# Where a two-layer encoder kernel issues its adding DMAs, builds its operand differences, and computes its last gates

## The chip, the cores and the metric

One core of a Trainium2 chip runs the whole kernel in one launch. The metric is device time in microseconds (us) of that launch. Engines are named as in the profile: PE is TensorE (matrix multiply), DVE is VectorE, ACT is ScalarE, POOL is GpSimd, SP is SyncE, which here only issues DMAs. Each engine works through its own instructions strictly in order; semaphores tie the engines together.

## The reference

The input x is 512 tokens by 1024, in float32. Layer 0 is a pooling mixer of inner width 2048 in 4 groups of 512:

```
hn = rms_norm(x)
v, gate = split(hn @ w_in)                       # 1024 -> 2 x 2048
p[g] = mean of v[g] over the last 2, 4, 8, 16 tokens - v[g]
x = x + ((p[g] @ w_grp[g]) * scale * silu(gate)) @ w_out
```

Layer 1 is a gated linear recurrence (HGRN2) of 16 heads of 128, followed by a final norm:

```
q, f, i, gate = split(rms_norm(x) @ w_in)        # 1024 -> 4 x 2048
o = recurrence over tokens, decay from f, key from f, value i, query q
x = x + (rms_norm(o, per head) * silu(gate)) @ w_out
out = rms_norm(x)
```

## The kernel before, in words

**Products.** Every product keeps nearly full float32 precision: each operand is split into a rounded high part (ACT copies it, line 98) and a low remainder (DVE subtracts, line 99), and `mm3` (lines 130 to 132) issues three matmuls per step of the contraction. Weights arrive in pieces of 512 KB: SP loads `wraw` (three buffers), ACT makes `whi`, DVE makes `wlo` (six buffers each). Results gather in four PSUM banks named `mm` and four named `a`.

**Layer 0** runs over four groups g of 512 channels. `values(g)` projects and DVE scales into `v`; `pool(g)` forms the window sums by doubling, one DVE add per doubling (line 305), into a tile `win` with two buffers, of which POOL must first clear the 16 columns ahead of the tokens (line 304); the next add reads those columns. `project_out` adds the group before into the residual h. `gates0(g)` projects the gate; its last step `gs` is a POOL multiplication (line 323). `mixed(g)` multiplies by `w_grp`. The row norm is not applied to the operand but afterwards: its factor `rn_l` (line 278, POOL) is spread over a tile by eight small matmuls (line 198) in the midst of the first gate product, and every layer 0 result waits for it.

**Layer 1** runs over four groups of four heads: `inputs(g)` forms the values, `heads` the weights within blocks and the states, `attend` the outputs, `gates1` the gates, `gated` their product, `prepare(g + 1)` decay, key and query of the next group, `add_out` the output product of the group before.

**A seven-product scheme.** The values of groups 2 and 3 are computed together by `inputs2`, which treats tokens, contraction and channels in halves and uses seven products of halves in place of eight. Three of these need sums of weight quarters; `weight_sums` builds four such sums (`wsum`, w4 to w7) in HBM with DMAs issued by POOL, 512 KB each, part of which add into their destination (`accum_op=ALU.add`). Four need differences of the activations; `differences` computes d and e (128 x 512 each, for j = 0 to 3), splits them, and stores all halves in HBM (`sums_d`); `again(i)` loads the one wanted into the buffers of the residual h, which is dead by then.

**What sets the order.** A planner orders the instructions of each engine before the program runs. It simulates the engines and at each moment issues, of what it holds to be ready, the instruction that was written earliest. Weight loads and splits are given a head start. An instruction without inputs to wait for can so stand far ahead of its place in the text. `weight_sums` is such a case: written inside layer 0, its 16 DMAs need nothing but each other.

Of the kernel before, what the change touches and what calls it, by code (L numbers as in the profile page):

```python
# [32 lines left out]
F32 = mybir.dt.float32  # L33
F32R = mybir.dt.float32r
# [3 lines left out]
ALU = mybir.AluOpType  # L38
PSUM = bass.MemoryType.PSUM

P = 128
D = 1024
T = 512
# [24 lines left out]
def trunk(ctx: ExitStack, tc: tile.TileContext, xT, x_d, par, ident_d, causal_d, mask_d, fg_d, w0_in, w0_grp, w0_out, w1_in, w1_out, out):  # L68
# [164 lines left out]
    def weight_sums(step):  # L233

        for g in PAIRS:
            w5, w6, w7, w4 = (wsum[g][i] for i in range(4))
            todo = (((w5, quarter(g, 0, 0), False), (w7, quarter(g, 0, 1), False)),
                    ((w5, quarter(g, 0, 1), True), (w7, quarter(g, 1, 1), True)),
                    ((w6, w5, False),), ((w6, quarter(g, 1, 1), True),),
                    ((w4, w6, False),), ((w4, quarter(g, 1, 0), True),))[step]  # L240
            for out_, in_, adding in todo:
                for r in range(0, 4 * P, 2 * P):
                    if adding:
                        nc.gpsimd.dma_start(out=out_[r:r + 2 * P], in_=in_[r:r + 2 * P], accum_op=ALU.add)
                    else:
                        nc.gpsimd.dma_start(out=out_[r:r + 2 * P], in_=in_[r:r + 2 * P])


    with tc.tile_pool(name="l0", bufs=1) as l0:
# [88 lines left out]
        zprev = None  # L338
        for g in range(NG):
            vs = values(g)  # L340
            if g:
                weight_sums(2 * g - 2)
            px = pool(g, vs)
            if zprev is not None and g < NG - 1:
                project_out(load_out(w0_out, g - 1), zprev)
            gts = gates0(g)
            if g:
                weight_sums(2 * g - 1)
            z = mixed(g, px, gts)
            if g == NG - 1:  # L350
                project_out(load_out(w0_out, g - 1), zprev)
            zprev = z
# [24 lines left out]
    def hgrn(ctx, general, h):  # L377
# [73 lines left out]


        own = [[(hi[:, t:t + 256], lo[:, t:t + 256]) for hi, lo in xs[k:k + 4]] for t in (0, 256) for k in (0, 4)]
        sums_d = dram.tile([2, 4, P, 2, T], F32, name=f"sums_{name}")
        v_d = dram.tile([TB, P, GC], F32, name=f"v_{name}")
        nrn = l1.tile([P, TB], F32, name="nrn")
        nc.gpsimd.tensor_scalar(out=nrn, in0=rn, scalar1=-1.0, scalar2=None, op0=ALU.mult)
        def differences():
            for j in range(4):
                t0, t4 = (small.tile([P, T], F32, name="t", tag="hg", bufs=2) for _ in range(2))  # L460
                for t, k in ((t0, j), (t4, 4 + j)):
                    nc.scalar.activation(out=t, in_=h[k], func=AF.Copy, scale=pp[:, C_NG1 + k:C_NG1 + k + 1])
                d, e = (small.tile([P, T], F32, name="d", tag="sq", bufs=2) for _ in range(2))
                u, w = slice(0, 256), slice(256, 512)
                nc.vector.tensor_tensor(out=d[:, u], in0=t4[:, w], in1=t0[:, w], op=ALU.subtract)
                nc.vector.scalar_tensor_tensor(out=d[:, w], in0=d[:, u], scalar=-1.0, in1=t0[:, u], op0=ALU.mult, op1=ALU.subtract)
                nc.vector.tensor_tensor(out=e[:, u], in0=t0[:, u], in1=t0[:, w], op=ALU.subtract)
                nc.vector.scalar_tensor_tensor(out=e[:, w], in0=t4[:, u], scalar=-1.0, in1=d[:, w], op0=ALU.mult, op1=ALU.subtract)
                first = halves(d, "z1", 4, l1)
                second = [const.tile([P, T], F32R, name="s", tag=f"h{k}", bufs=1) for k in (j, 4 + j)]  # L470
                split(e, *second)
                for i, pair in enumerate((first, second)):
                    for c, x in enumerate(pair):
                        nc.scalar.dma_start(out=sums_d[i, j, :, c], in_=x.bitcast(F32))

        def again(i):

            out = []
            for j in range(4):
                x = const.tile([P, 2, 256], F32R, name="s", tag=f"h{4 * (i % 2) + j}", bufs=1)  # L480
                nc.sync.dma_start(out=x.bitcast(F32), in_=sums_d[i // 2, j, :, :, (i % 2) * 256:(i % 2) * 256 + 256])
                out.append((x[:, 0], x[:, 1]))
            return out

        def inputs2(g):

            def pieces(src):
                v = src.rearrange("(k p) n -> p k n", p=P)
                out = []
                for i in range(0, 4, 2):
                    hi, lo = piece(v[:, i:i + 2])
                    out += [(hi[:, 0], lo[:, 0]), (hi[:, 1], lo[:, 1])]
                return out
            def product(accs, x, w):
                for b, acc in enumerate(accs):  # L500
                    t = slice(b * P, (b + 1) * P)
                    for k, ((xh, xl), (wh, wl)) in enumerate(zip(x, w)):
                        mm3(acc, xh[:, t], xl[:, t], wh, wl, k == 0, k == 3)

            two = lambda: [ps.tile([P, T], F32, name="mm", tag="mm", bufs=4) for _ in range(2)]
            v = l1.tile([P, TB, GC], F32, name="vn", tag="vn", bufs=1)
            v1 = [l1.tile([P, GC], F32, name="v1", tag="gs", bufs=4) for _ in range(TB)]
            s = again

            def plus(out, acc, x):  # L510
                nc.vector.tensor_tensor(out=out, in0=acc, in1=x, op=ALU.add)

            def times(x, by, t):
                nc.scalar.activation(out=x, in_=x, func=AF.Copy, scale=by[:, t:t + 1])

            a = two()
            product(a, own[0], pieces(quarter(g, 0, 0)))
            for b in range(2):
                nc.scalar.copy(out=v[:, 2 + b], in_=a[b])
            a = two()  # L520
            product(a, own[1], pieces(quarter(g, 1, 0)))
            for b in range(2):
                plus(v[:, b], a[b], v[:, 2 + b])
                times(v[:, b], rn, b)
            c = two()
            product(c, s(0), pieces(wsum[g][0]))
            s2 = s(1)
            a = two()
            product(a, s2, pieces(wsum[g][1]))
            s3 = s(2)  # L530
            for b in range(2):
                plus(v1[b], a[b], v[:, 2 + b])
            a = two()
            product(a, s3, pieces(wsum[g][2]))
            s4 = s(3)
            for b in range(2):
                plus(v[:, 2 + b], a[b], v1[b])
                plus(v1[2 + b], c[b], v[:, 2 + b])
                plus(v1[b], c[b], v1[b])
                times(v1[2 + b], nrn, 2 + b)  # L540
                nc.scalar.dma_start(out=v_d[2 + b], in_=v1[2 + b])
            a = two()
            product(a, own[3], pieces(wsum[g][3]))
            for b in range(2):
                plus(v[:, 2 + b], a[b], v[:, 2 + b])
                times(v[:, 2 + b], rn, 2 + b)
            a = two()
            product(a, s4, pieces(quarter(g, 1, 1)))
            for b in range(2):
                plus(v1[b], a[b], v1[b])  # L550
                times(v1[b], nrn, b)
                nc.scalar.dma_start(out=v_d[b], in_=v1[b])
            return v
# [61 lines left out]
        def group(g, prepare, heads, zs):  # L615
# [2 lines left out]
            first, last = g == 0, g == NG - 1  # L618
            v = inputs(g)
            if last:  # L620
                wg = load_in(w1_in, 3 * DI + g * GC)
                gts = gates1(wg, (0, 1))
                attend = heads(g, v, lambda: gts.extend(gates1(wg, (2, 3))))
                wo = load_out(w1_out, g - 1)
                add_out(wo, zs, (0,))
                ons = [attend(n) for n in range(GT)]
                add_out(wo, zs, (1,))
            elif first:
                attend = heads(g, v)
                turn()  # L630
                differences()
                wg = load_in(w1_in, 3 * DI + g * GC)
                gts = gates1(wg, (0, 1))
                ons = [attend(n) for n in range(GT)]
                gts += gates1(wg, (2, 3))
            else:
                attend = heads(g, v)
                add_out(load_out(w1_out, g - 1), zs)
                ons = [attend(n) for n in range(GT)]
                gts = gates1(load_in(w1_in, 3 * DI + g * GC), range(GT))  # L640
            now = [gated(g, n, ons[n], gts[n], last) for n in range(2)]
            if not last:
                prepare(g + 1)
            now += [gated(g, n, ons[n], gts[n], last) for n in range(2, GT)]
            if last:
                add_out(wo, zs, (2, 3))
            return now

        def finish(zs):
# [315 lines left out]
```

## Time and profile before

| | |
|---|---|
| time, median of 3 runs | 879.32 us (877.96 to 882.0) |
| profiled execution: its own time, its span | 877.26 us, 875.3 us |
| PE busy | 820.3 us (94%) |
| DVE, ACT, POOL busy | 574.3 us (66%), 294.4 us (34%), 163.5 us (19%) |
| DMA moved | 103.18 MB, mean 118 GB/s |
| chain that ended last | PE 74%, DVE 11%, issue 7%, DMA 4% |

Busy is the share of the span in which the engine executes. The chain that ended last is followed back from the last instruction, step by step, to whatever released it. "issue" is time in which an engine waited for nothing that the profile shows.

### The profile page before, as it was taken

The page shows a single profiled execution, that of the slowest core. Times are in us where ns is not written, and L with a number is a line of the kernel's source. Part 1 is how long each engine was busy: PE and PEld are TensorE (multiplying, and loading weights), DVE is VectorE, ACT ScalarE, POOL GpSimd, SP SyncE. Part 2 cuts the span into 40 slices and gives each one's busy share as a digit, 9 for nine tenths or more (in the row PEclk, how much of TensorE's full clock was granted, in tenths as well). Part 3 has the DMA queues.
Part 4 walks back from the last instruction along what each step waited for, and adds up shares of the span by engine and source line. Part 5 has one row for each costly group of instructions (what it writes and reads, how often), then busy time and mean ns, then how long its engine had stood idle before and what let it go on. Part 6 is the DMA issues. An engine that isn't in the chain of part 4 may idle for free.

```text
span 875.3 us, 10353 instructions
## 1 busy us (share of the span) xinstructions
PE 820.3 (94%) x3878; PEld 683.9 (78%) x3878; DVE 574.3 (66%) x881; ACT 294.4 (34%) x500; POOL 163.5 (19%) x214
## 2 busy tenths in 40 slices
PE   8707999999999999999999999999998999998995
PEld 6506888888888888888788878888876888887884
DVE  3405784467368656579847996437997654896764
ACT  4502422322242324442545223324244243313321
POOL 1112100200110202226013430032410012242300
PEclk9957999999999999999999999999999999999999
DMA  9982422322242314513373333212358342212202
GB/s 319 308 213 54 130 91 92 103 69 97 97 144 78 108 59 160 177 49 97 121 258 103 96 97 97 73 33 89 97 181 273 123 145 77 89 56 80 85 1 100
DMA packets 50091, 103.18 MB, mean 118 GB/s; under 512 B 3888, under 2 KB 8240, under 8 KB 49968
## 3 DMA queue, kind: packets, MB, share of 16 engines
q1 hardware_dynamic: 41248, 83.90, 29.0%
q0 software_dynamic: 2880, 8.39, 4.1%
q10 hardware_dynamic: 5904, 10.15, 3.2%
q8 instruction: 32, 0.52, 0.2%
q14 instruction: 27, 0.22, 0.1%
HBM read 92.99 MB, written 17.83 MB: 127 GB/s over the span
## 4 chain that ended last, share of the span: by engine, by line
PE 74%; DVE 11%; issue 7%; DMA 4%; POOL 1%; ACT 1%; POOLq 0%; DVEq 0%; SPq 0%; ACTq 0%
PE mm L131 22%; PE mm L130 22%; PE mm L132 22%; DVE r L718 3%; DVE wlo L99 3%; PE a L773 2%; DMA wsum<-wsum 1%; PE a L751 1%; PE a L775 1%; DMA wraw<-wsum 1%; DMA wraw<-in_w1i 1%; PE a L734 1%; ACT whi L98 1%; DMA s<-sums_fac 1%; DVE q L722 1%
## 5 line engine op out<-in xcount | busy, mean ns | idle before, releaser
L130 PE MATMUL mm<-xh,whi 128*128 128x512 f32 x624 | 245.0, 393 | 1.9 <-ACT whi L98 1.9
L131 PE MATMUL mm<-xl,whi 128*128 128x512 f32 x624 | 243.8, 391 | 0.0
L132 PE MATMUL mm<-xh,wlo 128*128 128x512 f32 x624 | 243.7, 391 | 0.0
L98 ACT CAST whi<-wraw 128x1024 fp32r<-128x1024 f32 (+1 forms) x146 | 147.7, 1025 | 239.6 <-PE mm L131 111.8
L99 DVE TENSOR_TENSOR wlo<-wraw,whi 128x1024 fp32r<-128x1024 f32 (+1 forms) x146 | 180.2, 1258 | 52.9 <-ACT whi L98 51.0
L130 PEld LDWEIGHTS mm<-xh,whi 128*128 128x128 f32 x624 | 117.5, 188 | 26.7 <-ACT whi L98 2.6
L132 PEld LDWEIGHTS mm<-xh,wlo 128*128 128x128 f32 x624 | 117.6, 188 | 25.4 <-DVE wlo L99 0.7
L131 PEld LDWEIGHTS mm<-xl,whi 128*128 128x128 f32 x624 | 117.6, 188 | 24.0
L718 DVE RECIPROCAL r<-r 128x512 f32<-128x512 f32 x16 | 53.4, 3338 | 0.0
L130 PE MATMUL mm<-zh,whi 128*128 128x512 f32 x128 | 49.8, 389 | 0.0
L131 PE MATMUL mm<-zl,whi 128*128 128x512 f32 x128 | 49.8, 389 | 0.0
L132 PE MATMUL mm<-zh,wlo 128*128 128x512 f32 x128 | 49.8, 389 | 0.0
L407 DVE TENSOR_TENSOR ht<-mm,ht 128x512 f32<-128x512 f32 x32 | 22.0, 688 | 30.1 <-PE mm L132 30.0
L592 POOL TENSOR_TENSOR ro<-mo,mhalf 128x4 f32<-128x4 f32 x16 | 16.2, 1014 | 134.5 <-DVE mo L590 134.5
L224 DVE TENSOR_TENSOR h<-mm,h 128x512 f32<-128x512 f32 x32 | 21.9, 688 | 28.3 <-PE mm L132 28.0
L323 POOL TENSOR_TENSOR gs<-gt,sg 128x512 f32<-128x512 f32 x16 | 21.9, 1373 | 87.6 <-ACT sg L321 87.6
L130 PE MATMUL mm<-whi,z1h 128*128 128x512 f32 x96 | 37.9, 395 | 0.0
L580 POOL TENSOR_TENSOR gs<-fz,s 128x512 f32<-128x512 f32 x16 | 22.4, 1403 | 81.5 <-ACT s L578 81.3
L131 PE MATMUL mm<-wlo,z1h 128*128 128x512 f32 x96 | 37.5, 390 | 0.0
L132 PE MATMUL mm<-whi,z1l 128*128 128x512 f32 x96 | 37.5, 390 | 0.0
L293 DVE TENSOR_TENSOR v<-mm,rb 128x512 f32<-128x512 f32 x16 | 10.8, 687 | 38.5 <-ACT rb L204 30.8
L131 PE MATMUL mm<-wlo,xh 128*128 128x512 f32 x88 | 34.5, 392 | 0.8 <-DVE wlo L99 0.8
(177 smaller groups left out, 1287.2 us busy)
## 6 DMA issues: line engine op xcount, KB each, us to landing
wraw<-in_w1i SPq DMA_DIRECT2D x62, 512.0 KB, 4.1
wraw<-in_w0i SPq DMA_DIRECT2D x28, 512.0 KB, 4.6
wraw<-in_w0o SPq DMA_DIRECT2D x16, 512.0 KB, 3.9
wraw<-in_w1o SPq DMA_DIRECT2D x16, 512.0 KB, 4.5
wsum<-in_w1i POOLq DMA_DIRECT2D x12, 512.0 KB, 7.0
wraw<-in_w0g SPq DMA_DIRECT2D x8, 512.0 KB, 4.0
s<-sums_fac SPq DMA_DIRECT2D x16, 256.0 KB, 4.3
wraw<-wsum SPq DMA_DIRECT2D x8, 512.0 KB, 4.1
```

Source lines behind the costliest of these rows:

```text
L98: nc.scalar.copy(out=hi, in_=src)
L99: nc.vector.tensor_tensor(out=lo, in0=src, in1=hi, op=ALU.subtract)
L130: nc.tensor.matmul(out, lh, rh, start=start, stop=False)
L131: nc.tensor.matmul(out, lh, rl, start=False, stop=False)
L132: nc.tensor.matmul(out, ll, rh, start=False, stop=stop)
L224: nc.vector.tensor_tensor(out=h[n], in0=acc, in1=h[n], op=ALU.add)
L323: nc.gpsimd.tensor_tensor(out=gs, in0=gt, in1=sg, op=ALU.mult)
L407: nc.vector.tensor_tensor(out=ht[b][:, c], in0=acc, in1=ht[b][:, c], op=ALU.add)
L580: nc.gpsimd.tensor_tensor(out=gs, in0=gt, in1=sg, op=ALU.mult)
L592: nc.gpsimd.tensor_tensor(out=ro[:, :, 0], in0=mo, in1=mhalf[:, :TB], op=ALU.pow)
L718: nc.vector.reciprocal(out=r, in_=r)
L773: nc.tensor.matmul(o[:, b], Ads[pr][:, j, t], v[:, b, n * P:(n + 1) * P], start=True, stop=b == 0)
```

## The change

1. `weight_sums` has four steps in place of six and is called once in each group of layer 0, after `gates0(g)`. Step 0 copies (8 DMAs of 512 KB), steps 1, 2 and 3 only add (8, 4 and 2 DMAs): 22 DMAs in place of 16, and 14 of them add in place of 8. No DMA reads `wsum` as a source any more. Each is passed to `tc.keep_in_program_order`, which makes the planner place it behind the POOL instruction written just ahead of it.
2. `differences` moves from group 0 of layer 1 (behind `turn`) to group 1 (behind `attend`, ahead of the gates). The two halves of e are split and stored; the two halves of d are split into the same buffers afterwards and stay on chip in `diff`. `inputs2` uses `diff` for its first two difference products and loads only the last two (8 loads in place of 16, 8 stores in place of 16, 256 KB each, now in one contiguous 2 KB run per partition).
3. In the last group all four gates come ahead of `heads`; `add_out` of the group before, four blocks of tokens, fills the places between: block 0 inside `heads`, block 1 before `attend`, block 2 after it, block 3 at the end. Before, two gates stood inside `heads`, block 0 before `attend`, block 1 after it, and blocks 2 and 3 at the end.

```diff
 def weight_sums(step):
     for g in PAIRS:
         w5, w6, w7, w4 = (wsum[g][i] for i in range(4))
-        todo = (((w5, quarter(g, 0, 0), False), (w7, quarter(g, 0, 1), False)),
-                ((w5, quarter(g, 0, 1), True), (w7, quarter(g, 1, 1), True)),
-                ((w6, w5, False),), ((w6, quarter(g, 1, 1), True),),
-                ((w4, w6, False),), ((w4, quarter(g, 1, 0), True),))[step]
+        b11, b12, b21, b22 = (quarter(g, i, j) for i in range(2) for j in range(2))
+        todo = (((w5, b11), (w6, b11), (w4, b11), (w7, b12)), ((w5, b12), (w6, b12), (w4, b12), (w7, b22)),
+                ((w6, b22), (w4, b22)), ((w4, b21),))[step]
...
+                    tc.keep_in_program_order(nc.gpsimd.dma_start(out=out_[r:r + 2 * P], in_=in_[r:r + 2 * P], **kind))
...
-            if g:
-                weight_sums(2 * g - 2)
             px = pool(g, vs)
...
             gts = gates0(g)
-            if g:
-                weight_sums(2 * g - 1)
+            weight_sums(g)
             z = mixed(g, px, gts)
...
-                first = halves(d, "z1", 4, l1)
-                second = [const.tile([P, T], F32R, name="s", tag=f"h{k}", bufs=1) for k in (j, 4 + j)]
-                split(e, *second)
-                for i, pair in enumerate((first, second)):
-                    for c, x in enumerate(pair):
-                        nc.scalar.dma_start(out=sums_d[i, j, :, c], in_=x.bitcast(F32))
+                for i, (x, half, k) in enumerate(((e, u, j), (e, w, 4 + j), (d, u, j), (d, w, 4 + j))):
+                    s = const.tile([P, 2, 256], F32R, name="s", tag=f"h{k}", bufs=1)
+                    split(x[:, half], s[:, 0], s[:, 1])
+                    if i < 2:
+                        nc.scalar.dma_start(out=sums_d[i, j], in_=s.bitcast(F32))
+                    else:
+                        diff[i - 2].append((s[:, 0], s[:, 1]))
...
             if last:
-                wg = load_in(w1_in, 3 * DI + g * GC)
-                gts = gates1(wg, (0, 1))
-                attend = heads(g, v, lambda: gts.extend(gates1(wg, (2, 3))))
+                gts = gates1(load_in(w1_in, 3 * DI + g * GC), range(GT))
                 wo = load_out(w1_out, g - 1)
-                add_out(wo, zs, (0,))
+                attend = heads(g, v, lambda: add_out(wo, zs, (0,)))
+                add_out(wo, zs, (1,))
                 ons = [attend(n) for n in range(GT)]
-                add_out(wo, zs, (1,))
+                add_out(wo, zs, (2,))
```

## Rows read from the trace of the kernel before

**Rows 1.** Waits of PE: engine, line, what ended the wait: us, times, longest
```profile
PE a L198 <- POOL rn_l L278: 31.0, 1, 31.0
PE a L734 <- ACT kt L742: 1.8, 1, 1.8
PE mm L130 <- DMA s<-sums_fac: 1.4, 1, 1.4
```
**Rows 2.** Stretches: us, busy us (instructions) by engine, PE clock, DMA share, GB/s
```profile
88.00:110.00 22.00, 22.00 (x99) 18.22 (x98) 17.34 (x22) 10.64 (x14) 3.17 (x5) 1.00 0.42 137
...
418.00:440.00 22.00, 19.97 (x135) 17.17 (x134) 18.08 (x45) 12.07 (x22) 0.79 (x1) 1.00 0.43 136
...
792.00:814.00 22.00, 19.65 (x118) 17.00 (x117) 14.58 (x23) 7.82 (x13) 5.88 (x4) 1.00 0.25 80
```
**Rows 3.** Timeline of POOL: start, us, instruction, [idle before, what ended it]
```profile
1.43 1.98 POOL L246 DMA_DIRECT2D wsum<-in_w1i  x3 [0.28 <-issue]
8.86 0.57 POOL L246 DMA_DIRECT2D wsum<-in_w1i  x1 [5.44 <-issue]
...
22.20 0.91 POOL L244 DMA_DIRECT2D wsum<-in_w1i  x1 [8.26 <-issue]
32.30 0.88 POOL L244 DMA_DIRECT2D wsum<-in_w1i  x1 [9.18 <-issue]
...
69.33 0.91 POOL L244 DMA_DIRECT2D wsum<-in_w1i  x1 [7.43 <-issue]
70.02 1.40 POOL L278 TENSOR_TENSOR rn_l<-ms,mhalf 128x4 f32<-128x4 f32 x1
```
**Rows 4.** Timeline of DVE, the input of the norm factor
```profile
32.10 0.17 DVE L276 TENSOR_SCALAR ms<-ss 128x4 f32<-128x4 f32 x1 [6.92 <-ACT xt L269]
```
**Rows 5.** Timeline of PE in the first 80 us
```profile
10.49 0.50 PE L130 MATMUL mm<-xh,whi 128*128 128x512 f32 x1 [1.78 <-ACT whi L98]
...
71.47 2.08 PE L198 MATMUL a<-ident,rn_l 128*128 128x128 f32 x8 [31.03 <-POOL rn_l L278]
...
73.77 0.63 PE L131 MATMUL a<-xl,whi 128*128 128x512 f32 x1
```
**Rows 6.** DMA queues from 12 to 37 us: packets, MB, share of 16 engines
```profile
q1 hardware_dynamic: 2701, 6.04, 63.3%
q0 software_dynamic: 900, 2.01, 38.5%
```
**Rows 7.** Line 244, all eight adding DMAs, from issue to landing
```profile
DMA to landing us min/median/max: 5.6/6.4/9.8
```
**Rows 8.** Line 244, the one issued at 22.20 us alone
```profile
DMA to landing us min/median/max: 9.8/9.8/9.8
```
**Rows 9.** Line 246, the three copies issued from 1.43 us
```profile
DMA to landing us min/median/max: 7.1/8.5/9.8
```
**Rows 10.** Timeline of POOL later in layer 0
```profile
96.80 1.30 POOL L323 TENSOR_TENSOR gs<-gt,sg 128x512 f32<-128x512 f32 x1 [4.70 <-ACT sg L321]
...
170.96 1.30 POOL L323 TENSOR_TENSOR gs<-gt,sg 128x512 f32<-128x512 f32 x1 [4.71 <-ACT sg L321]
188.20 0.11 POOL L304 MEMSET win<- 128x16 f32 x1 [15.94 <-DVE win L305]
...
247.12 1.30 POOL L323 TENSOR_TENSOR gs<-gt,sg 128x512 f32<-128x512 f32 x1 [4.72 <-ACT sg L321]
```
**Rows 11.** Timeline of DVE in layer 0, groups 1, 2 and 3
```profile
116.01 0.69 DVE L305 TENSOR_TENSOR win<-win 128x512 f32<-128x512 f32 x1
...
192.18 1.49 DVE L305 TENSOR_TENSOR win<-win 128x512 f32<-128x512 f32 x2
...
199.02 3.49 DVE L99 TENSOR_TENSOR wlo<-wraw,whi 128x1024 fp32r<-128x1024 f32 x3
...
262.82 2.21 DVE L305 TENSOR_TENSOR win<-win 128x512 f32<-128x512 f32 x3
```
**Rows 12.** Timeline of PE, third step of the first product with w_out
```profile
202.92 0.39 PE L131 MATMUL mm<-zl,whi 128*128 128x512 f32 x1
```

More of the change, by code (lines that the diff above doesn't have):

```diff
@@ L236, in weight_sums @@
             w5, w6, w7, w4 = (wsum[g][i] for i in range(4))
-            todo = (((w5, quarter(g, 0, 0), False), (w7, quarter(g, 0, 1), False)),
-                    ((w5, quarter(g, 0, 1), True), (w7, quarter(g, 1, 1), True)),
-                    ((w6, w5, False),), ((w6, quarter(g, 1, 1), True),),
-                    ((w4, w6, False),), ((w4, quarter(g, 1, 0), True),))[step]
-            for out_, in_, adding in todo:
+            b11, b12, b21, b22 = (quarter(g, i, j) for i in range(2) for j in range(2))
+            todo = (((w5, b11), (w6, b11), (w4, b11), (w7, b12)), ((w5, b12), (w6, b12), (w4, b12), (w7, b22)),
+                    ((w6, b22), (w4, b22)), ((w4, b21),))[step]
+            for out_, in_ in todo:
                 for r in range(0, 4 * P, 2 * P):
[L243 to L246, printed above, removed]
+                    kind = dict(accum_op=ALU.add) if step else {}
+                    tc.keep_in_program_order(nc.gpsimd.dma_start(out=out_[r:r + 2 * P], in_=in_[r:r + 2 * P], **kind))
     with tc.tile_pool(name="l0", bufs=1) as l0:
@@ L453, in hgrn @@
         own = [[(hi[:, t:t + 256], lo[:, t:t + 256]) for hi, lo in xs[k:k + 4]] for t in (0, 256) for k in (0, 4)]
-        sums_d = dram.tile([2, 4, P, 2, T], F32, name=f"sums_{name}")
+        diff = [[], []]
+        sums_d = dram.tile([2, 4, P, 2, 256], F32, name=f"sums_{name}")
         v_d = dram.tile([TB, P, GC], F32, name=f"v_{name}")
@@ L479, in again @@
             for j in range(4):
-                x = const.tile([P, 2, 256], F32R, name="s", tag=f"h{4 * (i % 2) + j}", bufs=1)
-                nc.sync.dma_start(out=x.bitcast(F32), in_=sums_d[i // 2, j, :, :, (i % 2) * 256:(i % 2) * 256 + 256])
+                x = const.tile([P, 2, 256], F32R, name="s", tag=f"h{4 * i + j}", bufs=1)
+                nc.sync.dma_start(out=x.bitcast(F32), in_=sums_d[i, j])
                 out.append((x[:, 0], x[:, 1]))
@@ L507, in inputs2 @@
             v1 = [l1.tile([P, GC], F32, name="v1", tag="gs", bufs=4) for _ in range(TB)]
-            s = again
+            s = lambda i: diff[i] if i < 2 else again(i - 2)
             def plus(out, acc, x):
@@ L630, in group @@
                 turn()
-                differences()
                 wg = load_in(w1_in, 3 * DI + g * GC)
@@ L635, in group @@
                 gts += gates1(wg, (2, 3))
+                l1.tile([P, 32], F32, name="pad2")
             else:
@@ L639, in group @@
                 ons = [attend(n) for n in range(GT)]
+                if g == 1:
+                    differences()
                 gts = gates1(load_in(w1_in, 3 * DI + g * GC), range(GT))
@@ L645, in group @@
             if last:
-                add_out(wo, zs, (2, 3))
+                add_out(wo, zs, (3,))
             return now
```

## The prediction
> **What bounds the kernel now.** I read the waits of PE first, because PE is busy for 94% of the span: its idle time is what an edit can win. One wait is larger than all the others together: PE stood 31.0 us before line 198, the spreading of `rn_l`, for POOL [rows 1]. Then POOL's own timeline in that stretch [rows 3]: it issues nothing but `wsum` DMAs from 1.43 us on, the last at 69.33 us, and `rn_l` follows directly at 70.02 us. Its input `ms` was there at 32.3 us [rows 4]. So `rn_l` was late only because it stood behind 16 DMAs in POOL's queue. The planner held those to be quick: had it simulated waits like these, `rn_l`, which is written earlier, would have come in between.
>
> Next, how POOL issues such DMAs, because the change issues more of them. Three copies go out within 2 us; the fourth waits until 8.86 us, just after the first has landed (1.43 + 7.1 = 8.5) [rows 3, 9]. An adding DMA waits for the adding one before it: that of 22.20 us lands 9.8 us later, at 32.0 us, and the next goes out at 32.30 us [rows 3, 8]. So POOL has at most three copies or one adding DMA of this size under way, and while it waits it executes nothing else. An adding DMA costs POOL its landing (5.6 to 9.8 us, median 6.4 [rows 7]) plus 0.3 us.
>
> Last, the stretches of layer 1: outside a few places PE never stops. Idle are 2.0 us in 418 to 440 us and 2.35 us in 792 to 814 us [rows 2].
>
> **Part 1a, the start.** Pinned behind the last `gs` of a group, no `wsum` DMA can stand ahead of `rn_l`. With `ms` at 32.3 us and 1.4 us of POOL, `rn_l` is there at 33.7 us. PE arrived at line 198 at 71.47 - 31.03 = 40.4 us [rows 5], so the gap goes entirely: 31.0 us. What is late next there is PE itself, and it gets faster too: from 12 to 37 us the DMA engines were full (63.3% + 38.5%), and the 38.5% were `wsum` [rows 6]. From 10.49 to 40.4 us PE had 102 matmuls of 512 columns (84 of the first four products, 18 of the gate) to do; in full flow 99 of them take 22 us [rows 2], so 22.7 us of the 30. The other 7.2 us were waits for weights and slow matmuls behind such waits, and 1.78 us more were lost just before 10.49 us. Weights that no longer share the DMA engines should remove most of it: I take 7 us, bounds 0 and 9. Behind the long gap, matmuls took 0.63 us in place of 0.39 [rows 5, 12]; I count 2 us for that stretch, which goes with the gap (0 to 3). Sum of the start: 40 us won, bounds 31 and 43.
>
> **Part 1b, what stands behind the DMAs now.** Each step's DMAs sit on POOL behind the last `gs` of the group, and behind them stand the memsets of `win` for the group that follows. These cannot go ahead: each needs a buffer that DVE gives back only in the middle of `pool(g + 1)`, and the planner, which held 16 DMAs to be quick, will hold 8 to be done before that.
> - Step 0, 8 copies behind the `gs` that ends at 98.1 us [rows 10]: three at once, then one for each landing; landings of the first three were some 2.1 us apart (8.5, 10.8, 12.7 us). POOL is free at about 98.1 + 7.1 + 4 x 2.1 + 0.6 = 114.2 us. DVE wants the cleared columns at 116.0 us [rows 11]. Cost nothing; with all landings at 9.8 us some 1 us late, which DVE's idle time takes.
> - Step 1, 8 adding DMAs behind the `gs` that ends at 172.26 us [rows 10]: seven full turns and an issue, 7 x 6.7 + 0.9 = 47.8 us, so POOL is free at 220.1 us on the old time axis. The memset that went at 188.20 us waits till then, and DVE's add at 192.18 us waits for it: 28.0 us. Behind this add stand, on DVE, the scaling of `v`, and the `wlo` splits at 199.02 us [rows 11], of which the first served the third step of `project_out`. PE can run on that far: its third matmul of that step would have started at 202.92 + 0.23 = 203.15 us [rows 12], and the split, 1.2 us long, now ends at 199.02 + 1.2 + 28.0 = 228.2 us. PE stalls for 25 us. With landings of 5.6 us it is 19.5 us, of 9.8 us 48.8 us. The matmuls behind this gap will be slow again: 1.5 us (0 to 3).
> - Step 2, 4 adding DMAs behind 248.42 us: 3 x 6.7 + 0.9 = 21.0 us, POOL free at 269.4 us. The last of the three adds at 262.82 us [rows 11] would have begun at about 264.3 us, so DVE is 5 us late; PE has finished splits and free banks for about 4 of these. I take 1 us; bounds 0 (5.6 us landings: 2.7 us late) and 11 (9.8 us landings: 15.3 us late).
> - Step 3, 2 adding DMAs, some 8 us of POOL near 303 us, ahead of `mixed(3)` and `project_out`, which do not use POOL. Nothing.
>
> The price of 6.7 us a turn rests on rows half of which come from a saturated stretch and half from one where PE stood still. The load beside step 1 (DMA share 0.42 in 88 to 110 us, the nearest stretch of normal flow [rows 2]) lies between, so I take the median.
>
> The Trainium skill, DMA: Bandwidth & Descriptors, section on the anatomy of one SWDGE DMA, gives a fit of 2.0 us plus the bytes over 436 GB/s. For 512 KB that is an estimate of 3.2 us; the trace disagrees, since not one adding DMA took under 5.6 us [rows 7]. By that rule a turn is 3.5 us, PE would stall 2.6 us in place of 25, and the kernel would come out at about 839 us.
>
> **Part 2, the differences.** DVE and ACT work moves out of group 0, where PE idled 2.0 us in 418 to 440 us [rows 2], in part because the causal copies stood behind it on DVE: I take 1 us won, bounds 0 and 2. It lands in group 1, in the output product, where PE has four full banks of work and finished splits; but each store must land before the d half can take its buffer, and ACT's queue, with weight copies, waits behind it: cost 0.5 us, bounds 0 and 4. Of the loads, the two that go were not waited for; the last two stay where PE waited 1.4 us for one [rows 1], with longer runs: 0.5 us won, bounds 0 and 1.4.
>
> **Part 3, the last gates.** Four gate products (21.8 us of PE) in front of the heads, in place of two, give DVE time to finish its reciprocals; the waits of 1.8 us and 0.6 us at line 734 should go: 2.35 us [rows 1, 2]. Against it, only one block of `add_out` in place of two is left at the end to cover the last splits, so up to 2 us may come back. I take 1 us won, bounds 2.35 won and 2 lost.
>
> Parts 2 and 3: 2 us won; bounds 6 won, 6 lost.
>
> **The sum**, against the profiled execution's own 877.3 us: 877.3 - 40 + 25 + 1.5 + 1 - 2 = 863 us. The median of the runs shown lies 2 us above that execution, well inside the range; I leave the forecast at 863.
>
> **Rivals.**
> - *POOL does not hold DVE.* The planner places the memsets between the DMAs, or the turns are short as by the fit above. For it: everything behind 71 us ran at full pace, so a planner's small shift suffices. Against: `rn_l` stood behind all 16, and no row has a turn under 5.9 us. Time: 877.3 - 40 - 2 = 835 us, up to 839.
> - *Slower: the adding DMAs crawl.* Beside the weight loads each turn takes what it took at 22.20 us, 10.1 us. Then step 1 costs 48.8 us and step 2 11 us: 877.3 - 40 + 48.8 + 11 + 1.5 - 2 = 897 us. With turns of c the two stalls are about 7c - 22 and 3c - 19; the 40 us are eaten from c = 8.1 us on. For it: two of the eight landings. Against: those stood in full queues.
> - *The differences don't move.* The planner takes the earliest ready instruction; the inputs of `differences` are ready at once, so they may float back into group 0. Then part 2 is worth nothing and the time is 864 us, inside the forecast.
>
> **How the numbers follow.** The forecast with its own range of 853 to 873 us (landings of 5.6 to 7 us, the start's gain 36 to 43): 0.55. POOL not or half in the way, 832 to 853 us: 0.27, and 0.04 below. Between 873 and 884 us 0.08, the slow rival above it 0.06. A range of 832 to 876 us holds somewhat over 8 in 10. Two runs of this kernel cannot be told apart within 0.5%, 4.4 us. Faster than 875 us: 0.88; within: 0.06; slower: 0.06.
>
> **What will show it.** Right: line 198 runs before 36 us and PE's wait for `rn_l` is gone; POOL shows eight adding DMAs in a row behind the gates of group 1, some 6.7 us apart; a wait of DVE at line 305 for POOL's memset, and a gap of PE of about 25 us in `project_out` of group 2. Wrong: memsets of `win` between those DMAs, turns under 5 us, or a DVE that had its splits done ahead of the add. Also wrong if PE still waits for weights before 30 us, or if the heads of the last group still wait for `kt`.

## The result, and the profile of the changed kernel

The changed kernel takes 870.57 us, the median of 20 executions (864.12 to 879.03), against 879.54 us (875.54 to 884.61) for the kernel before. Two of the 20, 878.45 and 879.03 us, lie over 1.5% above the fastest and are left out of the ratio, which is 0.9888, 95% interval 0.9864 to 0.9912. The kernel is faster by 1.1%, and 7.6 us over the forecast of 863. The profiled execution is the one of 878.45 us (span 876.6), and that of before lies 2 us under its median: the two traced executions differ by 1.2 us, in favour of before. So terms are read place by place, the gaps found are looked for again in the traces of other executions, and verdicts on a part rest on ratios to before. Line numbers of layer 0 are lower by two than before, and line 734 is line 733.

The waits of PE (engine, line, what ended the wait: us, times, longest), to be held against [rows 1]:

```profile
PE mm L130 <- ACT whi L98: 26.9, 2, 23.5
PE mm L130 <- DVE fz L574: 7.3, 1, 7.3
PE mm L132 <- DVE wlo L99: 4.9, 2, 2.6
PE mm L130 <- DVE vn L509: 3.4, 2, 2.6
PE mm L130 <- DMA s<-sums_fac: 0.7, 2, 0.4
```

The 31.0 us for `rn_l` and the 1.8 us for `kt` are gone. In their place stand 23.5 us for a weight copy, and a wait that before does not have at all, 7.3 us for `fz` of layer 1's gates.

PE's timeline (start, us, instruction, idle before it and what ended it):

```profile
31.61 1.05 PE L198 MATMUL a<-ident,rn_l 128*128 128x128 f32 x8
...
184.07 0.80 PE L130 MATMUL mm<-zh,whi 128*128 128x512 f32 x1 [23.54 <-ACT whi L98]
...
187.91 0.79 PE L132 MATMUL mm<-zh,wlo 128*128 128x512 f32 x1 [2.61 <-DVE wlo L99]
...
591.05 0.80 PE L130 MATMUL mm<-xh,whi 128*128 128x512 f32 x1 [7.33 <-DVE fz L574]
...
592.08 0.63 PE L132 MATMUL mm<-xh,wlo 128*128 128x512 f32 x1
592.50 0.63 PE L130 MATMUL mm<-xh,whi 128*128 128x512 f32 x1
```

Line 198 runs 39.9 us earlier than in [rows 5], and 0.63 us matmuls at twice the usual spacing (592.08, 592.50) follow the gaps, as they did there. The busy time by stretch shows what that costs (columns as in [rows 2]):

```profile
154.00:176.00 22.00, 6.53 (x29) 5.07 (x27) 0.00 (x0) 0.00 (x0) 3.57 (x4) 0.70 0.51 76
176.00:198.00 22.00, 11.32 (x35) 8.51 (x35) 16.73 (x26) 5.64 (x7) 1.92 (x13) 0.60 0.57 140
...
418.00:440.00 22.00, 21.62 (x140) 18.97 (x139) 10.75 (x31) 7.60 (x14) 1.31 (x1) 1.00 0.28 94
572.00:594.00 22.00, 14.67 (x68) 12.09 (x67) 14.04 (x27) 11.27 (x20) 1.07 (x1) 0.82 0.48 167
792.00:814.00 22.00, 22.00 (x121) 18.95 (x120) 18.99 (x24) 9.57 (x15) 7.35 (x5) 1.00 0.46 153
```

From 154 to 176 us DVE and ACT executed nothing and POOL nothing but four DMA issues; PE stands from 160.5 us on, and the granted clock averages 0.70 and 0.60 of 2.4 GHz, so part of these stretches ran at the 1.2 GHz level. The stretches at 418 and 792 us, with 2.0 and 2.35 us idle before, are nearly full.

POOL, against [rows 3, 10]:

```profile
21.09 1.01 POOL L276 TENSOR_TENSOR rn_l<-ms,mhalf 128x4 f32<-128x4 f32 x1 [19.95 <-DVE ms L274]
...
71.05 0.57 POOL L244 DMA_DIRECT2D wsum<-in_w1i  x1 [1.92 <-issue]
71.60 0.13 POOL L302 MEMSET win<- 128x16 f32 x1
...
129.89 0.94 POOL L244 DMA_DIRECT2D wsum<-in_w1i  x1
138.88 0.91 POOL L244 DMA_DIRECT2D wsum<-in_w1i  x1 [8.05 <-issue]
148.74 0.88 POOL L244 DMA_DIRECT2D wsum<-in_w1i  x1 [8.95 <-issue]
...
178.95 0.90 POOL L244 DMA_DIRECT2D wsum<-in_w1i  x1 [5.10 <-issue]
179.51 0.50 POOL L302 MEMSET win<- 128x16 f32 x2
```

Eight adding DMAs in a row, the first turns 9.0 and 9.9 us, the others 6.0 to 6.1, and only then the memsets: POOL is held for 49.6 us behind the gates of group 1. DVE (its timeline, as in [rows 11]) comes to its add right then, and to the splits 6.6 us after it; the release is put down to the memset of `v` that POOL does beside that of `win`:

```profile
180.00 1.49 DVE L303 TENSOR_TENSOR win<-win 128x512 f32<-128x512 f32 x2 [30.25 <-POOL v L290]
...
186.63 3.49 DVE L99 TENSOR_TENSOR wlo<-wraw,whi 128x1024 fp32r<-128x1024 f32 x3
```

Where the two traces drift apart, by the start of the same PE work (minus: the changed kernel is ahead): -42.3 us at the first `project_out`; -12.4 at its group-1 end; -4.0 at the end of layer 0; -8.3 at the heads of group 1; +3.1 at the output heads of group 2; 0.0 at the last phase; +1.3 at the end of the span.

### The profile page after: what moved, and what is told of

It reads as the page before. It is cut to its first block, busy times and chain, and to the rows that moved or that the text cites. A ratio compares the mean times of both kernels' runs of the same rounds, so it can differ in the third digit from the quotient of the medians.

```text
span 876.6 us, 10351 instructions
## 1 busy us (share of the span) xinstructions
PE 822.4 (94%) x3878; PEld 687.2 (78%) x3878; DVE 574.9 (66%) x889; ACT 296.5 (34%) x508; POOL 167.7 (19%) x220
## 4 chain that ended last, share of the span: by engine, by line
PE 74%; issue 10%; DVE 7%; DMA 4%; POOL 2%; ACT 2%; ACTq 0%; POOLq 0%; DVEq 0%; SPq 0%
PE mm L130 22%; PE mm L132 22%; PE mm L131 22%; DVE wlo L99 2%; DVE r L717 2%; DMA wraw<-in_w1i 1%; DMA s<-sums_fac 1%; PE a L772 1%; POOL wsum L244 1%; PE a L750 1%; DMA wraw<-wsum 1%; PE a L733 1%; PE a L774 1%; ACT whi L98 1%; DVE win L303 1%
## 5 line engine op out<-in xcount | busy, mean ns | idle before, releaser
L130 PE MATMUL mm<-xh,whi 128*128 128x512 f32 x624 | 246.3, 395 | 10.7 <-DVE fz L574 7.3
L130 PE MATMUL mm<-zh,whi 128*128 128x512 f32 x128 | 51.2, 400 | 23.5 <-ACT whi L98 23.5
L130 PEld LDWEIGHTS mm<-zh,whi 128*128 128x128 f32 x128 | 24.8, 194 | 29.0 <-ACT whi L98 24.0
L303 DVE TENSOR_TENSOR win<-win 128x512 f32<-128x512 f32 x24 | 17.4, 727 | 41.8 <-POOL v L290 30.2
L98 ACT CAST ph<-p 128x512 fp32r<-128x512 f32 x16 | 9.9, 620 | 92.9 <-DVE p L307 92.9
```

Source lines behind the costliest of these rows:

```text
L98: nc.scalar.copy(out=hi, in_=src)
L130: nc.tensor.matmul(out, lh, rh, start=start, stop=False)
L303: nc.vector.tensor_tensor(out=nxt[:, 16:], in0=cur[:, 16:], in1=cur[:, 16 - step:16 + T - step], op=ALU.add)
```

## The experiments

The theory to be tested: POOL's hold by adding DMAs reaches PE through DVE's one add; the rest of the miss is the place of `differences`. Rivals: the adding traffic itself slows the weights; for `differences`, what costs is the keeping on chip, where a store must land before its buffer is taken again.

**The memset away from POOL**, all else as changed:

```diff
-                        nc.gpsimd.memset(nxt[:, 0:16], 0.0)
+                        nc.vector.memset(nxt[:, 0:16], 0.0)
```

> Edit: the memset of the 16 columns ahead of win (line 302 of the changed kernel) is issued by DVE instead of POOL; the 22 wsum DMAs stay where they are, as long as they are. Theory (POOL held by adding DMAs holds DVE, and DVE holds PE): the PE gaps of 23.5 + 2.6 us in project_out of group 2 and of 3.4 + 2.3 us in group 3 vanish with the slow matmuls behind them (about 30 and 8 us in the profiled execution), while 32 short memsets cost DVE some 0.1 us each; time 870.6 - 32 to 38 = 833 to 839 us. Rival (the wsum traffic of 11.5 MB slows the weight loads, since PE waits for ACT's weight copy): the traffic is the same, so the gaps stay and the time stays at 868 to 872 us.

Measured: 841.03 us, ratio to before 0.9554 (0.9534 to 0.9574). That is 2 us above the expected range, which took losses read from the 878.45 us execution off the median. POOL is held as long as before, its DMAs at the same pace (timeline of POOL):

```profile
129.72 0.95 POOL L244 DMA_DIRECT2D wsum<-in_w1i  x1
...
178.18 0.90 POOL L244 DMA_DIRECT2D wsum<-in_w1i  x1 [5.30 <-issue]
178.75 0.59 POOL L290 MEMSET v<- 128x16 f32 x4
```

but DVE clears its columns itself, in 0.07 us, in the midst of it (timeline of DVE), and the longest wait of PE that is left is the one in layer 1:

```profile
151.20 0.07 DVE L302 MEMSET win<- 128x16 f32 x1
```

```profile
PE mm L130 <- DVE fz L574: 8.0, 1, 8.0
```

PE takes 21.5 us for the second `project_out` and 130.6 us from there to the end of layer 0, both as in before. So the same traffic, without the wait, costs layer 0 nothing: the wait of DVE for the memset is the whole stall, some 30 us of the kernel. The traffic rival falls.

**Copies in place of adds.** Every step copies, so the weight sums are left out and the values of groups 2 and 3 are others:

```diff
-                    kind = dict(accum_op=ALU.add) if step else {}
+                    kind = {}
```

> Edit: the 14 adding DMAs are plain copies of the same size from the same source to the same place (the weight sums are left out, so the values of groups 2 and 3 are others). Theory (an adding DMA goes out only when the one before has landed, three copies at once): the 8 DMAs of step 1 hold POOL about as long as step 0 does, 16 us instead of 50, and the gaps in groups 2 and 3 vanish: 833 to 839 us. Rival (number and bytes of DMAs count, not the adding): the hold stays at 40 us and more, time 865 to 872 us.

Measured: 841.04 us, ratio 0.9557 (0.9534 to 0.9581), again 2 us above the range expected. The timeline of POOL in step 1:

```profile
130.43 1.68 POOL L244 DMA_DIRECT2D wsum<-in_w1i  x3
...
143.29 0.57 POOL L244 DMA_DIRECT2D wsum<-in_w1i  x1 [0.79 <-issue]
```

The same bytes go out in 13.4 us, as three copies may be under way at once, and no wait is left in layer 0. The hold belongs to adding DMAs that take turns, not to eight DMAs.

**Part 2 undone** (differences in group 0, all four stored and loaded again, as before; parts 1 and 3 stay):

```diff
...
                 turn()
+                differences()
...
-                if g == 1:
-                    differences()
...
```

> Edit: part 2 undone (differences back in group 0, all four stored and loaded again), parts 1 and 3 kept. New theory, from the trace of the changed kernel: in group 1 the DVE and ACT queues run through differences while the four gate products wait to be taken out of PSUM, and PE stands 7.3 us, 8.4 us with the slow matmuls behind it; group 0 loses again what it had gained, some 3 to 4 us: net 4 to 5 us faster, 865 to 867 us. What the prediction said (part 2 is worth 1 us): 871 to 872 us.

Measured: 867.93 us, ratio 0.9825 (0.9783 to 0.9866). The wait for `fz` is gone, the gaps of layer 0 stay (23.3 and 2.6 us, then 3.2 and 1.8). By the ratios part 2 costs 0.0063 of 879.5, 5.5 us; the two intervals just overlap, so its size needed the quieter base below.

**The changed kernel once more**, for a second trace.

> The changed kernel itself once more, for a second profile: its first profiled execution took 878.5 us, its median is 870.6 us. Theory: the gaps in groups 1, 2 and 3 are there again, and the 8 us between executions are in how long the first two adding DMAs of a step take beside weight loads (8.7 and 9.6 us against 5.7). Rival: the spread comes from elsewhere (the first 30 us, layer 1) and the gap in group 2 is the same within 1 us.

It took 875.9 us. The long gap is 24.1 us, again; group 3 differs (timeline of POOL in step 2):

```profile
236.24 0.89 POOL L244 DMA_DIRECT2D wsum<-in_w1i  x1
...
257.91 0.89 POOL L244 DMA_DIRECT2D wsum<-in_w1i  x1 [5.45 <-issue]
```

Four issues in 21.7 us, where the first trace has 25.1 us with turns of 9.1 and 10.0 us; PE loses 4.5 us from the end of the group-1 product to the end of layer 0 in place of 8.4. Up to there the two executions differ by the turns of step 2. The gap in group 2 is the same within 1 us, as the rival had it. What the faster executions do otherwise is not shown: this one, too, lies 5 us above the median.

**Part 2 undone with the memset on DVE**, that is e1's edit and part 2's together, to have its price where no adding DMA disturbs:

> Edit: the memset of win on DVE (as in e1) and part 2 undone (as in e2). Theory (the two losses are independent: POOL's hold about 30 us, part 2 a net 6.9 us by the milestones of e1 and e2, where group 1 to group 2 loses 11.5 us with part 2 and group 0 wins 4.7): 841.0 - 7 = 834 us, faster than the kernel before and the changed one. What the prediction said of part 2 (worth 1 us): 842 us.

Measured: 834.17 us, ratio 0.9468 (0.944 to 0.9497). Against 841.03 part 2 costs 6.9 us; the two kernels ran on different chips, and by their ratios to before it is 7.6 us.

**Place or keeping?** On the same base, once the new code called in group 0, and once the old code, all four stored, called in group 1:

```diff
                 turn()
+                differences()
...
-                if g == 1:
-                    differences()
```

> Edit against e1: differences is called in group 0 behind turn, as in the kernel before, but still keeps the halves of d on chip. Theory (the place in group 1, ahead of the gates, is what costs): the PE gap of 8 us in group 1 goes, group 0 loses its 4 to 5 us, 833 to 836 us. Rival (each half of d waits for the store of the half of e in the same buffer, so ACT stands, wherever it is done): a gap comes in group 0 instead, and the time stays at 838 us or above.

Measured: 833.38 us, ratio 0.9468 (0.9434 to 0.9502).

```diff
-                for i, (x, half, k) in enumerate(((e, u, j), (e, w, 4 + j), (d, u, j), (d, w, 4 + j))):
...
+                first = halves(d, "z1", 4, l1)
+                second = [const.tile([P, T], F32R, name="s", tag=f"h{k}", bufs=1) for k in (j, 4 + j)]
+                split(e, *second)
+                for i, pair in enumerate((first, second)):
...
```

> Edit against e1: differences stays in group 1, but stores all halves as the kernel before did, in buffers of their own, and all four are loaded again. Theory A (its tiles t share two buffers with the gates' fz, and the planner sets fz behind it on DVE, so PE finds no free PSUM bank): the gap of 8 us before the products of prepare stays, 839 to 843 us. Theory B (the d halves wait for the stores of the e halves): no such waits now, the gap shrinks under 3 us, 833 to 836 us.

Measured: 839.72 us, ratio 0.9537 (0.9503 to 0.957). The stretch from 545 to 575 us (columns as in [rows 2]), first of the kernel with the work kept on chip but in group 0, then of that with all stored but in group 1:

```profile
545.00:575.00 30.00, 30.00 (x138) 24.88 (x137) 24.44 (x41) 12.44 (x18) 7.92 (x10) 1.00 0.34 106
```

```profile
545.00:575.00 30.00, 22.40 (x90) 18.19 (x89) 19.08 (x43) 10.97 (x18) 6.79 (x10) 0.83 0.43 152
```

PE is full in the one and 7.6 us short, at a clock of 0.83, in the other. The place costs; keeping two of four on chip is harmless, and is worth nothing that these runs can tell (833.38 against 834.17 us, with overlapping intervals).

**How the place costs.** In the changed kernel the work of `differences` runs just ahead of group 1's gates (timelines of DVE and of ACT):

```profile
564.00 0.42 DVE L462 TENSOR_TENSOR d<-t 128x256 f32<-128x256 f32 x1
...
572.42 0.43 DVE L99 TENSOR_TENSOR s<-d,s 128x256 fp32r<-128x256 f32 x1 [1.61 <-ACT s L98]
...
588.05 1.23 DVE L99 TENSOR_TENSOR wlo<-wraw,whi 128x1024 fp32r<-128x1024 f32 x1 [1.51 <-ACT whi L98]
...
590.32 0.68 DVE L574 TENSOR_TENSOR fz<-mm,rb 128x512 f32<-128x512 f32 x1
```

```profile
571.99 0.41 ACT L98 CAST s<-d 128x256 fp32r<-128x256 f32 x1 [1.63 <-DMA sums_fac<-s]
...
586.97 1.04 ACT L98 CAST whi<-wraw 128x1024 fp32r<-128x1024 f32 x1 [2.29 <-DMA wraw<-in_w1i]
```

The pieces pass back and forth between ACT and DVE for 26 us, with pauses for stores; the first `fz` reads a finished bank of PE only at 590.32 us. Until then `fz` has no buffer: its tag, `hg`, has two, and `t0` and `t4` of `differences` take both in turn, four times. One kernel gives them other buffers, again with the memset on DVE (`general` is false in the layer that runs):

```diff
-                t0, t4 = (small.tile([P, T], F32, name="t", tag="hg", bufs=2) for _ in range(2))
+                t0, t4 = (small.tile([P, T], F32, name="t", tag="hg", bufs=2) if general else l1.tile([P, T], F32, name="t", tag="r", bufs=2) for _ in range(2))
```

> Edit against e1: the tiles t of differences take the two buffers of r (idle in this stretch) in place of the two that fz uses. Theory A: fz no longer waits for the buffers of t, the planner sets it earlier, the gap of 8 us shrinks under 3 us, 832 to 836 us. Theory B (waits for stores): the gap stays, 839 to 842 us.

Measured: 836.5 us, ratio 0.9495 (0.9462 to 0.9528); 4.5 us of the 6.9 are back, by the ratios 5.2 of 7.6. Its waits of PE:

```profile
PE a L733 <- DVE z L604: 6.7, 1, 6.7
PE mm L130 <- DVE fz L574: 1.1, 1, 1.1
```

The wait for `fz` falls from 8.0 to 1.1 us, so the shared buffers make that wait. But PE now waits 6.7 us at the heads of group 2, with DVE without a pause from 590 to 620 us (30.00 us busy of 30). With the buffers shared DVE is as full there (29.89 us of 30), and PE, which comes later, does not wait at these heads. That DVE has no room for more work in this stretch is thus a second cause read from the traces, not one that a run shows by itself. How the rest divides was not taken further.

**Parts 2 and 3 alone, and part 1 alone.**

> The changed kernel with part 1 undone: the weight sums in the two calls per group of before, with their copies and adds as before; the differences in group 1 with two of four kept on chip, and the order of the last group, stay. My prediction gave these two parts -2 us, so about 877.5 against 879.5. What the experiments so far give instead: the place in group 1 costs about 7 us, the last group's order gives back 2.5 to 3, so 883 to 884, with a wait of the PE of 6 to 8 us in group 1 that ends on DVE fz, and the 31 us gap of the start and the short gaps of layer 0 as before.

Measured: 885.36 us, ratio 1.0053 (1.0036 to 1.007): slower by 4.7 us. Its waits of PE:

```profile
PE a L198 <- POOL rn_l L278: 33.4, 1, 33.4
PE mm L130 <- DVE fz L579: 8.4, 1, 8.4
```

> The changed kernel with parts 2 and 3 undone: differences in group 0 and all four stored, the last group's gates in two halves round its heads as before; the weight sums in four steps. My prediction would give 863 + 2 = 865 by its sum (start -40, hold +26.5, group 3 +1). With the terms as measured (start -42.3, hold +29.9, group 3 +4.6 to +8.4): -8 to -4 us, so 871 to 875, or, by the ratio of the kernel in which only part 2 is undone (0.9825) and 2.5 to 3 us for the last group, 867. No gap in group 1.

Measured: 868.96 us, ratio 0.9849 (0.9819 to 0.9879): 13.3 us won (10.7 to 15.9) against the 881.01 us of before on that chip. Its longest waits of PE are those of the changed kernel's layer 0, and none is for `fz`:

```profile
PE mm L130 <- ACT whi L98: 25.3, 2, 21.2
PE mm L132 <- DVE wlo L99: 4.4, 2, 2.6
```

Against it and against the kernel without part 2 (0.9825), part 3 wins some 2 us (the intervals overlap); on the trace of the changed kernel it is 3.1 us, from the heads of group 2's output to the last phase.

**Adds of half the size.**

```diff
-                for r in range(0, 4 * P, 2 * P):
+                for r in range(0, 4 * P, P if step else 2 * P):
...
-                    tc.keep_in_program_order(nc.gpsimd.dma_start(out=out_[r:r + 2 * P], in_=in_[r:r + 2 * P], **kind))
+                    tc.keep_in_program_order(nc.gpsimd.dma_start(out=out_[r:r + (P if step else 2 * P)], in_=in_[r:r + (P if step else 2 * P)], **kind))
```

> The changed kernel with every adding DMA of steps 1 to 3 cut into two of half the rows (256 KB each), the same bytes in 16, 8 and 4 DMAs. What is asked is what sets the turn of an adding DMA, 6.0 us alone and 9 to 10 beside weight loads. If the turn is mostly a fixed cost of one DMA and only one is under way at a time, step 1 takes 16 turns of 4 to 6 us, POOL is held 65 to 95 us in place of 49.6, and the kernel takes 885 to 915 us. If the turn goes with the bytes (about 3 us for a half), the hold stays at 50 and the time at 870. If half-sized DMAs let two be under way at once, the hold falls below 45 us and the time to 860 or less.

Measured: 852.74 us, ratio 0.9685 (0.9669 to 0.9701). The timeline of POOL in step 1, and the line that gives the 16 DMAs' time to landing:

```profile
129.80 2.57 POOL L244 DMA_DIRECT2D wsum<-in_w1i  x3
135.80 0.84 POOL L244 DMA_DIRECT2D wsum<-in_w1i  x1 [3.43 <-issue]
...
160.07 0.82 POOL L244 DMA_DIRECT2D wsum<-in_w1i  x1 [1.17 <-issue]
160.59 0.46 POOL L302 MEMSET win<- 128x16 f32 x2
...
DMA to landing us min/median/max: 4.7/5.1/8.5
```

The same line of the changed kernel, for its eight in step 1:

```profile
DMA to landing us min/median/max: 5.7/5.8/9.5
```

A half takes nearly as long as a whole, but three go out at once, the next when one has landed. The hold falls from 49.6 to 30.7 us, the long gap from 23.5 to 4.7 us (the 2.6 us behind it stay), and the gaps of group 3 go. The third of the expected outcomes, by more than expected.

The fastest kernels run are those with the memset on DVE and the differences in group 0: 833.38 and 834.17 us, 5.3% under the kernel before.

## Why the prediction was right, and where it was not

| step | predicted, us | shown, us |
|---|---|---|
| 1a, the start | -40 | -42.3 |
| 1b step 1, gap of PE | +25 | +26.1 (waits of 23.5 and 2.6) |
| slow matmuls behind it | +1.5 | +3.8 |
| step 2, group 3 | +1 | +7.7 to +8.4 in three traces, +4.5 in a fourth |
| part 2 | -1 | +5.5 to +7.6 |
| part 3 | -1 | -2 to -3 |

The forecast is 7.6 us low, and 870.57 lies 2.4 us inside the upper end of its range, 853 to 873. That range was worked out from the turns and the start alone; part 2 missed by 6 to 9 us and step 2 by 3 to 7, so that it still holds is in part luck.

**Part 1a** held: the gap went entirely, line 198 runs at 31.61 us, and what the prediction priced at 9 us beside the 31.0 came to 11.3. PE waits for no weights before that line, where before it did so for some 4 us.

**Part 1b** held in its mechanism, place and size. POOL was free 15.6 us after the `gs` of step 0, where 16.1 were worked out, and nothing waited; it was held 49.6 us in step 1 where 47.8 were worked out, with a mean turn of 7.0 us in place of 6.7. The wait was named at line 305, the `win` add being meant, which is line 303 of the changed kernel. The first rival, a POOL that does not hold DVE, falls: its 835 to 839 us are what comes out only once the memset is taken off POOL (841). The slow rival needed turns of 8.1 us or more throughout; only the first two of step 1 and two of step 2 were as long. The Trainium skill, DMA: Bandwidth & Descriptors, section on the anatomy of one SWDGE DMA (a DMA that GpSimd issues), stood behind a turn of 3.5 us. The runs disagree: the adding DMAs of step 1 took 5.7 us at the least for 512 KB, and 4.7 us at the least for 256 KB, where an estimate by its fit is 2.6 us.

**Step 2** was mis-sized. "PE has finished splits and free banks for about 4 of these" gave it credit that it had not: PE waited 3.4 us for a weight copy and 2.3 us for a split, and matmuls were slow behind both. A hold of 21.0 us was expected, and the two traces of the changed kernel have 25.6 and 22.2. The traces with part 2 undone and with part 1 alone agree with the longer one: turns of 8.8, 9.9 and 6.2 us and of 9.0, 10.6 and 6.2 us, and PE loses 7.7 and 8.3 us. As the price is what exceeds a cover, a turn longer by one or two us counts three times.

**Part 2** is the step that failed: "It lands in group 1, in the output product, where PE has four full banks of work and finished splits" and "cost 0.5 us". The stores that the prediction watched for do pause ACT, but they are not the cause: the kernel that stores all halves in group 1, from buffers of their own, has a wait for `fz` of 7.6 us, and the one that keeps two on chip in group 0 has none. The prediction looked at what PE has in front of it, and not at what the moved work takes in common with the next work: the two `hg` buffers that the gates need and, as far as the traces tell, DVE's room in that stretch. Group 0 won 4.3 us where 1 was expected (418 to 440 us is nearly full), and 11.4 us were lost from the heads of group 1 to the output heads of group 2: 7.3 us of gap, some 2.5 us of slow matmuls (192 took 46.35 us in place of 43.81), the other 1.6 us were not followed. "The differences don't move" was no answer either: they did.

**Part 3** held, with two or three times the size; the waits for `kt` at line 734 are gone, and 0.4 us came back in the last product.

By the ratios, part 1 alone won 13.3 us (10.7 to 15.9) against a predicted sum of 12.5, and parts 2 and 3 cost 4.7 us (3.2 to 6.2) against a predicted gain of 2. These 6.7 us, less the 0.8 us that part 1 won more, and the 2.2 us by which the median of before lies over the execution that the sum started from, make 8.1 us, about the miss of 7.6.

That part 1 comes out at its sum does not show that its terms do. The traces give it less at the end of layer 0: 4.0 and 7.6 us with the changed kernel, 7.4 us with part 1 alone (start -42.3, step 1 +26.6, step 2 +8.3). The executions traced explain some of that: the one of before, 877.26 us, is 3.7 us faster than the median on the chip where part 1 ran alone, and the others, 878.45, 875.9 and 870.52 us, lie at the slower end of their kernels' times. Which term is smaller in the executions that have no trace stays open. The turns of adding DMAs are the candidate, since they differ between the traces, and since the changed kernel's 20 executions spread over 15 us while 5 of the kernel whose DVE does not wait for them spread over 1 us (840.23 to 841.23).

## What to carry to other kernels

When slow DMAs are put behind a milestone on an engine that also computes, list what stands behind them on that engine; one 0.1 us memset that another engine waits for made 30 us of stall, and moving that memset was worth more than the whole change. When work is moved "under" a long stretch of PE, ask which buffers and which engine's free time it shares with the work that comes right after it, not only how much PE has to do. And a price that is the excess over a cover moves in multiples of its input: give it a wide range. Where an engine is held by its own DMAs, look at how many DMAs it can have under way, not only at their bytes: the same bytes in halves won 18 us here.

## What was not expected of the hardware

- Adding DMAs of 512 KB go one at a time, in the changed kernel's step 1 with turns of 6.0 to 9.9 us, but of 256 KB three at a time, each 4.7 to 8.5 us from issue to landing; eight copies of 512 KB were issued in 13.4 us, three at a time. The packets on POOL's queue order these cases, where bytes do not: 2176 for the eight adding DMAs of step 1 (line below, 128 to 185 us: packets, MB, share of 16 engines), that is 272 each; 1152 for the eight copies and 2304 for the sixteen halves, that is 144 each.

```profile
q0 software_dynamic: 2176, 4.19, 47.9%
```

  Three of 144, 432 packets, were under way at once; two of 272, 544, never. The trace of before has a mixed case in POOL's timeline:

```profile
12.99 0.96 POOL L244 DMA_DIRECT2D wsum<-in_w1i  x1 [3.56 <-issue]
```

  This adding DMA went out beside one copy, 416 packets in all, just after the landing of another copy at 12.6 us, with which there would have been 560. In none of the traces do such counts give more than 432 under way, and each issue that waited for room and not for data would have made 544 or more. So a bound between 432 and 544 packets accounts for all cases; that is an estimate from these counts, and no run changed the packets alone.
- An adding DMA keeps the queues busier than a copy that moves as much: from 128 to 185 us the DMA engines were busy for 0.72 of the time at 167 GB/s with adds (memset on DVE), for 0.49 at 171 GB/s with copies (columns as in [rows 2]):

```profile
128.00:185.00 57.00, 57.00 (x253) 47.20 (x252) 39.28 (x62) 15.51 (x19) 8.71 (x13) 1.00 0.72 167
```

```profile
128.00:185.00 57.00, 57.00 (x253) 47.18 (x253) 39.53 (x55) 15.73 (x19) 6.82 (x21) 1.00 0.49 171
```
